# A hybrid attention block on one core: h written over the transposed x, row copies moved to another ring, and three steps set some ticks later

## The chip, the core and the metric

The kernel runs on one core of one Trainium2 chip. The metric is the device time of one execution in microseconds (us); the time of a version is the median of its runs. The core has a matrix engine (TensorE, PE in the rows), a vector engine (VectorE, DVE), a scalar engine (ScalarE, ACT), a general engine (GpSimd, POOL) and a sync engine (SyncE, SP) whose only work here is to issue transfers. Each engine takes its own instructions in order; semaphores hold them back where they depend on one another.

## What is computed

One residual block for a sequence of 1024 tokens and 1024 channels, in float32. Cut to what matters here:

```python
mod = silu(c) @ ada_w + ada_b                       # adaLN: six vectors of 1024
shift1, scale1, gate1, shift2, scale2, gate2 = split(mod, 6)
h = rms_norm(x, pre_mix_w) * (1 + scale1) + shift1
proj = h @ w_in                                     # q, k, v, gates of both branches
o_a = gla_chunked(...)                              # 4 heads, gated and normed
o_d = gated_delta_chunked(...)                      # 8 heads (GDN), gated and normed
merged = sigmoid(m_a) * (o_a @ w_branch_gla) + sigmoid(m_d) * (o_d @ w_branch_gdn)
x = x + gate1 * rms_norm(merged @ w_out, post_mix_w)
h2 = rms_norm(x, pre_mlp_w) * (1 + scale2) + shift2
x = x + gate2 * rms_norm(square(relu(h2 @ mlp_w1)) @ mlp_w2, post_mlp_w)
```

## The kernel before

**Precision.** A product in float32 is made of three matmuls in a rounded format: a high part times a high part, low times high, high times low. So every operand is split: ACT casts the high part (`hH`, `wH`, `oH`), DVE subtracts it from the original to get the low part (`hL`, `wL`, `oL`). Where the weights come by an accumulating transfer, ACT writes the negated high part and POOL's queue adds the weights to it.

**Memory.** Most tiles come from four rings in SBUF: `w4` with 30 slots of 128x1024 floats, `wt` with 8, `hd` with 4, `sl` with 2 (lines 24, 75 to 78). A new tile takes a slot whose last tenant is released, and its first writer waits for every reader of that tenant, a transfer out of it among them.

**Order.** A clock of ticks counts the PE's work: `tick` (line 377) is called after every few matmuls, `at(n, fn)` (line 366) puts a step n ticks ahead, and `run_due` puts the steps that are due into the engines' queues at that place. A tick says only where an instruction stands in its engine's queue, not when it runs. For the stage of the branch products `st(t, fn)` counts ticks from `stage0`, and tables such as `gla_plan` (line 1588) list the steps.

**The start.** x comes in as eight row tiles, is normed and transposed by PE into `xT[0..7]`, one tile of channels each. The first two adaLN vectors (shift1 and scale1) are made in four passes, p = 0 to 3, each for the channels of two tiles. The weights of pass 0 lie in `hd` (`ada_load`, line 200), those of pass 1 in `sl` and `wt`, those of passes 2 and 3 in `w4`. A pass is: `ada_pe` (16 matmuls into one bank), `ada_out` (ACT copies the 128x512 result to a row tile `acc`), `ada_fin` (PE sums it into columns), `ada_cols` (DVE makes the columns `am1`, `sh1`), `high` (ACT writes `hH` of both tiles from `xT`), `low` (line 279: DVE writes `h` = xT * am1 + sh1, then `hL` = h - hH, and SP stores `h` to HBM in `h_d`, where a later stage reads it). `first_tiles` (line 485) interleaves these passes with the first matmuls of h with the weights: `a_` (hH by high weights), `b_` (hH by low weights), `c_` (hL by high weights); the table `fill` gives the three groups that stand within each pass.

**The middle.** Then come key tiles, a triangular solve, branch gates, the four GLA heads, and the eight GDN heads (`gdn_head`, line 898), the last of which runs into the next stage. A GDN head ends with: `results` (ACT squares and copies the output to `ob`), `norm` and `scale` (DVE: a root in 11 small steps, then `ob` times it), `fin` (PE transposes `ob` half by half in four 128x128 pieces, DVE gates it into `sg`, printed as `si` in the rows), and a store to `od_d`. For head 6 these steps are set 27 ticks later (`end`), so that they stand in the products' stage, where they alternate with head 7's.

**The products.** `stage0` is the tick at which head 7's dense part ends and the branch products begin. Each of the three branches (GLA's, a gate's, GDN's) is made of seven half-size products in the order P2, P1, P6, P7, P4, P5, P3 (line 1755), 8 ticks each (48 matmuls with 512 columns in four groups of 12; the first two groups need the weights of half h = 0, the others those of h = 1). Operands are prepared by the plan: `x_cast`/`x_low` give `oH`/`oL`, `w_cast`/`w_low` the two parts of `wB` (halves h = 0 and 1). `split_raw` (line 1584) puts `w_cast` and, two ticks later where no accumulating transfer is used, `w_low`. P4 of the GLA branch starts at tick 32.

**adaLN's other four vectors** are summed on DVE throughout the heads, one piece every 12 ticks (`ada_sum`, line 1333), and closed by `ada_total` (line 1343): transposes and sums on DVE in two parts, one PE step 14 ticks later, DVE columns, and for the gates a row that goes to HBM.

Of the kernel before, what the change touches and what calls it, by code (L numbers as in the profile page):

```python
# [9 lines left out]
F32R = mybir.dt.float32r  # L10
# [40 lines left out]
def block_kernel(ctx: ExitStack, tc: tile.TileContext, x, c, ada_w, ada_b, pre_mix_w, post_mix_w,  # L51
# [9 lines left out]
    w4 = ctx.enter_context(tc.tile_pool(name="w4", bufs=1))  # L61
# [9 lines left out]
    def nm(p):  # L71
        uid[0] += 1
        return f"{p}{uid[0]}"
# [3 lines left out]
    def t4(shape=(128, 1024), dt=F32, p="t", tag="w4"):  # L77
        return w4.tile(list(shape), dt, tag=tag, name=nm(p), bufs=tag_bufs[tag])
# [4 lines left out]
    def pat(shape=(128, 512)):  # L83
        return pa.tile(list(shape), F32, tag="pa", name=nm("pa"))

    def dump(name, src, dst=None):
        if dbg and name in dbg:
            DMA.dma_start(dbg[name] if dst is None else dst(dbg[name]), src)
# [20 lines left out]
    def small(n, p="s", bufs=3, dt=F32):  # L109
        return sm.tile([128, n], dt, tag=f"{p}{n}", name=nm(p), bufs=bufs)  # L110
# [111 lines left out]
    xT = [t4(p="xT") for _ in range(8)]  # L222
# [21 lines left out]
    accs, pac, pcol = {}, {}, {}  # L244
# [7 lines left out]
                     start=(k < 4), stop=(k >= 4))  # L252

    def ada_out(p):
        accs[p] = t4((128, 512), p="acc")
        A.copy(accs[p], pac[p])

    def ada_fin(p):
# [11 lines left out]
    hH, hL, hs = [None] * 8, [None] * 8, [None] * 8  # L270
# [7 lines left out]

    def low(p):
        for d in (2 * p, 2 * p + 1):  # L280
            hs[d], hL[d] = t4(p="h"), t4(dt=F32R, p="hL")
            V.tensor_scalar(hs[d], xT[d], am1[:, d:d + 1], sh1[:, d:d + 1], ALU.mult, ALU.add)
            V.tensor_tensor(hL[d], hs[d], hH[d].bitcast(F32), ALU.subtract)
            DMA.dma_start(h_d[d // 2][d % 2], hs[d])
            dump("hT", hs[d], lambda t, d=d: t[d * 128:(d + 1) * 128, :])
# [80 lines left out]
    def at(dt, fn):  # L366
        agenda.append((clock[0] + dt, len(agenda) + uid[0] * 100000, fn))
        agenda.sort(key=lambda e: e[:2])
        uid[0] += 1
# [49 lines left out]
    def conv_w_later(raw_ap, shape, dh, dl, src=None):  # L419

        w = [None, None]

        def high():
            w[0] = t4(shape, F32R, "wH", "wt")
            A.copy(w[0], raw_ap)

        def low():
            w[1] = t4(shape, F32R, "wL", "wt")
            if src is None:
                V.tensor_tensor(w[1], raw_ap, w[0].bitcast(F32), ALU.subtract)  # L430
            else:
                A.activation(w[1], raw_ap, AF.Copy, scale=-1.0)
                G.dma_start(w[1], src, accum_op=ALU.add)

        at(dh, high)
        at(dl, low)
        return w
# [47 lines left out]
    def first_tiles():  # L485
# [27 lines left out]

        wk_low(0)
        low(0)
        V.tensor_tensor(wS[:, :, 32:64], raw_lba, wS[:, :, 0:32].bitcast(F32), ALU.subtract)
        wk_low(1)
# [6 lines left out]
        for p in range(1, 4):  # L524
            f = [lambda e=e: e[0](*e[1:]) for e in fill[p]]
            ada_pe(p)
            ada_out(p)
            f[0]()
            ada_fin(p)
            ada_cols(p)  # L530
            high(p)
            f[1]()
            f[2]()
            low(p)
            if p == 2:
                ahead[1] = next(ahead[0])
            a_(p)
# [153 lines left out]
    def r3(t, n=8):  # L691
        return t.rearrange("p (t q) -> p t q", t=n)
# [205 lines left out]
    def gdn_head(h, then=None):  # L898
# [163 lines left out]
                on(47 + late if hf else 35, lambda: results(hf, po))  # L1062

        late, end = (7, 27) if h == 6 else (0, 0)
        f_ = end + 6 if h == 7 else end

        def results(hf, po):
            if not hf:
# [264 lines left out]
    def ada_sum(i, k, raw):  # L1333
        with V.behind():
            if k == 0:
                adat[i] = t4(p="aacc", tag="hd")
                V.tensor_scalar(adat[i], raw, sc[:, k:k + 1], None, ALU.mult)
            else:
                V.scalar_tensor_tensor(adat[i], raw, sc[:, k:k + 1], adat[i], ALU.mult, ALU.add)
        if k == 7:  # L1340
            at(28 if i == 3 else 8, lambda: ada_total(i))

    def ada_total(i):

        _, b0, w0, dst = ADA[i]
        acc, bias, z = adat.pop(i), adab[:, b0:b0 + 8], {}
        t, r = t4(p="sqt"), small(32, "asr", 2)

        def part(hf):
            h_ = slice(hf * 512, (hf + 1) * 512)  # L1350
            with V.behind():
                V.transpose(t[:, h_], acc[:, h_])
                V.reduce_sum(r[:, hf * 16:(hf + 1) * 16], r3(t[:, h_], 16), axis=mybir.AxisListType.X)

        def total():
            z["ps"] = pat()
            T.matmul(z["ps"][:, 0:32], quad.rearrange("p a b -> p (a b)"), r, start=True, stop=True)

        def columns():
            o = small(8, "gcol", 1) if dst is None else dst  # L1360
            for c in range(4):
                q = slice(32 * c, 32 * c + 32)
                V.tensor_tensor(o[q], z["ps"][q, 0:32].rearrange("p (t c) -> p c t", c=4)[:, c], bias[q], ALU.add)
            if dst is None:
                V.tensor_tensor(o, o, vcol[:, w0:w0 + 8], ALU.mult)
                at(10, lambda: ada_row(i, o))
            elif dst is am2:
                V.scalar_tensor_tensor(am2, am2, 1.0, premlp, ALU.add, ALU.mult)

        part(0)  # L1370
        at(2, lambda: part(1))
        at(14, total)
        at(15, columns)

    def ada_row(i, g):
        ps, row = pat(), sm.tile([128, 256], F32, tag="gst", name=nm("grow"), bufs=3)[:, 0:128]
        T.transpose(ps[0:8, 0:128], g, ident)
        V.tensor_copy(row[0:8], ps[0:8, 0:128])
        ST.dma_start(gw_d[i // 3].rearrange("(r p) -> r p", p=128), row[0:8])
# [180 lines left out]
    A11, A12, A21, A22 = (0, 0), (1, 0), (0, 1), (1, 1)  # L1560
# [8 lines left out]
    def rows_of(r, gated=True):  # L1569

        for kp in range(2):
            r += [(25 + kp, "x_sum", Q21, Q21, "t2", kp),
                  (26 + kp, "x_cast", "P4", Q21, kp), (27 + kp, "x_low", "P4", Q21, kp),
                  (33 + kp, "x_cast", "P5", Q12, kp), (34 + kp, "x_low", "P5", Q12, kp),
                  (41 + kp, "x_cast", "P3", Q22, kp), (42 + kp, "x_low", "P3", Q22, kp)]
        for h in range(2):
            r += [(32 + 2 * h, "w_cast", "P5", A21, h), (36 + 2 * h, "w_low", "P5", A21, h),
                  (38 + 4 * h, "w_cast", "P3", A12, h), (44 + 3 * h, "w_low", "P3", A12, h)]
        for (cb, tb), t in (((0, 0), 13), ((1, 0), 37), ((1, 1), 45), ((0, 1), 53)):
            for h in range(2 if gated else 0):  # L1580
                r += [(t + 4 * h - 6, "load_s", cb, tb, h)]
        return sorted(r, key=lambda e: e[0])

    def split_raw(r, p, key, c0, c1, dma=True):
        for h, c_ in ((0, c0), (1, c1)):
            r += [(c_, "w_cast", p, key, h), (c_ + 1 + (not dma), "w_neg" if dma else "w_low", p, key, h)]

    def gla_plan():
        r = [(-19, "load_w", A12, True), (-16, "load_x", Q21, "wt"), (-11, "load_w", A11, True), (-5, "load_x", Q11),
             (-4, "load_x", Q12), (-3, "load_x", Q22), (-2, "load_w", A21), (1, "add_w", A21, A22), (8, "load_w", A22),  # L1590
             (21, "load_x", Q21)]
        split_raw(r, "P2", A12, -10, -7)
        split_raw(r, "P1", A11, -3, 1)
        split_raw(r, "P4", A22, 22, 25, False)
        for kp in range(2):
            r += [(-6 + kp, "x_cast", "P2", Q21, kp), (-5 + kp, "x_low", "P2", Q21, kp),
                  (-1 + kp, "x_cast", "P1", Q11, kp), (kp, "x_low", "P1", Q11, kp),
                  (1 + kp, "x_sum", Q12, Q12, Q11, kp), (3 + kp, "x_t2", kp), (5 + kp, "x_sum", Q11, "t2", Q11, kp),
                  (8 + kp, "x_cast", "P6", "t2", kp), (9 + kp, "x_low", "P6", "t2", kp),
                  (8 + 2 * kp, "w_sum", A11, A21, A11, kp), (10 + kp, "w_cast", "P6", A11, kp), (12 + kp, "w_low", "P6", A11, kp),  # L1600
                  (14 + kp, "w_sum", A12, A12, A11, kp), (15 + kp, "w_sum", A11, A22, A11, kp),
                  (17 + kp, "x_cast", "P7", Q11, kp), (18 + kp, "x_low", "P7", Q11, kp),
                  (19 + kp, "w_cast", "P7", A11, kp), (20 + kp, "w_low", "P7", A11, kp)]
        return rows_of(r)
# [651 lines left out]
    for n in range(len(seq)):  # L2256
        gi, key, c = seq[n]
        grp = GROUPS[gi]
        first, end = c == grp[0], c == grp[-1]
# [58 lines left out]
    for t in range(NT):  # L2318
        hf, to = t // 4, slice(t % 4 * 128, t % 4 * 128 + 128)
        end = t == NT - 1  # L2320
# [43 lines left out]
```

## Time and profile before

| what | us |
|---|---|
| median of 3 runs | 1916.46 |
| lowest and highest of them | 1913.89 and 1917.49 |
| the profiled execution | 1914.38 |
| its span, first to last instruction | 1912.7 |
| PE busy in the span | 1879.5 |

The profile is one execution. A row of the timeline has the start, the duration, the engine, the operation with what it writes and reads, the count, and in brackets the idle time just before it and what ended it. PEld is the loading of weights into the matrix engine, which runs beside the matmuls. Matmuls overlap, so the time that a group takes is read from the start of one row to the start of the next. Names have no buffer numbers in the profile; in the order of instructions they have, so that a tile can be followed there. All these instructions are recorded through one helper and so carry one line number; the tile names tell them apart.

### The profile page before, as it was taken

Reading aid. Unit: us, or ns where it says so; the run is one execution under the profiler, and the core shown is the slowest. Engines: PE = TensorE matmul, PEld = TensorE weight load, DVE = VectorE, ACT = ScalarE, POOL = GpSimd, SP = SyncE. Lnnn points to the kernel's source line nnn. Section 1 sums busy time; section 2 is a strip of 40 time slices with the busy share of each in tenths; the row PEclk is TensorE's granted clock in tenths of the full one; section 3 lists DMA queues with packets and bytes.
Section 4 is the critical chain, followed back from the end, with each engine's and each line's share of the span. In section 5 each row is a group of like instructions: output and inputs, shape, how many; then the busy total and the mean of one; then the engine's idle time right before and its main releaser. Section 6 shows DMA issues by size and latency. Waiting matters only on the chain.

```text
span 1912.7 us, 26562 instructions
## 1 busy us (share of the span) xinstructions
PE 1879.5 (98%) x10217; PEld 1576.4 (82%) x10217; DVE 1352.7 (71%) x2178; ACT 884.6 (46%) x1613; POOL 150.8 (8%) x140
## 2 busy tenths in 40 slices
PE   6999999999999999999999999999999999999998
PEld 4788888889898888888878888888888888888886
DVE  5564744769775666766788678667578886777887
ACT  5465324342432444444654556457544446443333
POOL 2020020110101000000101011000012120000001
PEclk9899999999999999999999999999999999999999
DMA  9485773122224444444869567436666758262425
GB/s 320 163 251 171 194 161 101 56 89 90 76 91 147 120 132 132 134 138 126 254 169 231 178 174 206 134 101 201 220 207 221 245 204 307 100 220 87 178 100 99
DMA packets 251567, 312.23 MB, mean 163 GB/s; under 512 B 72530, under 2 KB 178208, under 8 KB 251440
## 3 DMA queue, kind: packets, MB, share of 16 engines
q1 hardware_dynamic: 221936, 274.67, 44.8%
q0 software_dynamic: 13232, 20.85, 6.2%
q10 hardware_dynamic: 16272, 15.02, 2.4%
q8 instruction: 80, 1.31, 0.3%
q14 instruction: 47, 0.39, 0.1%
HBM read 230.10 MB, written 80.39 MB: 162 GB/s over the span
## 4 chain that ended last, share of the span: by engine, by line
PE 95%; DMA 2%; DVE 2%; ACT 1%; issue 0%; POOL 0%; DVEq 0%; ACTq 0%; SPq 0%; POOLq 0%
PE pm L38 62%; PE pa L38 33%; DMA wq<-in_w_branch_gla_dram 1%; DMA h_d<-h 1%; DMA vt<-in_c_dram 0%; DVE oL L38 0%; DVE rt L38 0%; ACT hH L38 0%; ACT ob L38 0%; DVE ob L38 0%; DVE hL L38 0%; DVE rs L38 0%; DVE ya L38 0%; ACT jk L38 0%; DVE wL L38 0%
## 5 line engine op out<-in xcount | busy, mean ns | idle before, releaser
L38 PE MATMUL pm<-hH,wH 128*128 128x512 f32 x864 | 286.3, 412 | 0.0
L38 PE MATMUL pm<-hL,wH 128*128 128x512 f32 x864 | 268.6, 392 | 0.0
L38 PE MATMUL pm<-hH,wL 128*128 128x512 f32 x864 | 267.2, 390 | 0.0
L38 PE MATMUL pm<-oH,wB 128*128 128x512 f32 x672 | 215.7, 395 | 0.0
L38 PE MATMUL pa<-w,yH 128*128 128x512 f32 (+1 forms) x696 | 212.3, 387 | 0.0
L38 PEld LDWEIGHTS pm<-hH,wL 128*128 128x128 f32 x864 | 162.1, 188 | 36.4
L38 PEld LDWEIGHTS pm<-hL,wH 128*128 128x128 f32 x864 | 162.2, 188 | 36.1
L38 DVE TENSOR_TENSOR w<-raw,w 128x512 fp32r<-128x512 f32 (+1 forms) x144 | 125.8, 876 | 49.4 <-ACT w L38 48.5
L38 PEld LDWEIGHTS pm<-hH,wH 128*128 128x128 f32 x864 | 145.1, 190 | 17.0
L38 PEld LDWEIGHTS pa<-w,yH 128*128 128x128 f32 x696 | 130.1, 188 | 26.8 <-DVE ya L38 0.4
L38 PEld LDWEIGHTS pm<-oH,wB 128*128 128x128 f32 x672 | 126.7, 189 | 26.4 <-DMA wB<-in_w_branch_gla_dram 0.4
L38 ACT CAST w<-raw 128x512 fp32r<-128x512 f32 (+1 forms) x144 | 99.3, 711 | 89.1 <-DVE raw L38 79.2
L38 PE MATMUL pa<-w,yL 128*128 128x512 f32 (+1 forms) x348 | 134.5, 387 | 0.0
L38 PE MATMUL pm<-oL,wB 128*128 128x512 f32 x336 | 131.3, 391 | 0.0
L38 PE MATMUL pa<-oB,w 128*128 128x512 f32 x480 | 111.4, 390 | 0.0
L38 ACT CAST wH<-raw 128x1024 fp32r<-128x1024 f32 x62 | 64.5, 1048 | 93.2 <-PE pm L38 45.9
L38 PEld LDWEIGHTS pa<-oB,w 128*128 128x128 f32 x480 | 89.8, 188 | 18.5
L38 DVE SCALAR_TENSOR_TENSOR cv<-pm,ccol,cv 128x1023 f32<-128x1023 f32 (+2 forms) x72 | 92.1, 1279 | 14.8 <-ACT cv L38 11.7
L38 DVE TENSOR_TENSOR wL<-raw,wH 128x1024 fp32r<-128x1024 f32 x62 | 76.2, 1233 | 35.6 <-ACT wH L38 35.5
L38 PE MATMUL pm<-oT,w 128*128 128x512 f32 x384 | 90.8, 389 | 0.0
L38 PE MATMUL pa<-oT,w 128*128 128x512 f32 x384 | 90.8, 389 | 0.0
L38 DVE TENSOR_TENSOR ya<-pa,ya 128x512 f32<-128x512 f32 (+1 forms) x83 | 56.0, 683 | 43.7 <-PE pa L38 43.7
(378 smaller groups left out, 3711.1 us busy)
## 6 DMA issues: line engine op xcount, KB each, us to landing
yL<-y_d SPq DMA_DIRECT2D x53, 512.0 KB, 7.5
raw<-in_mlp_w_dram SPq DMA_DIRECT2D x23, 1024.0 KB, 6.2
raw<-in_w_in_dram SPq DMA_DIRECT2D x18, 1024.0 KB, 7.3
raw<-in_w_in_dram SPq DMA_DIRECT2D x32, 512.0 KB, 4.8
araw<-in_ada_w_dram SPq DMA_DIRECT2D x32, 512.0 KB, 3.8
raw<-in_mlp_w_dram SPq DMA_DIRECT2D x18, 512.0 KB, 5.4
araw<-in_ada_w_dram SPq DMA_DIRECT2D x32, 256.0 KB, 6.0
sl<-sg_d SPq DMA_DIRECT2D x16, 512.0 KB, 7.9
```

What stands on the lines that cost most here:

```text
L38: r = fn(*args, **kw)
```

## The change

Five edits, and nothing else:

```diff
     def ada_out(p):
-        accs[p] = t4((128, 512), p="acc")
+        accs[p] = t4((128, 512), p="acc", tag="hd" if p else "w4")
         A.copy(accs[p], pac[p])
...
     def low(p):
         for d in (2 * p, 2 * p + 1):
-            hs[d], hL[d] = t4(p="h"), t4(dt=F32R, p="hL")
+            hs[d], hL[d] = xT[d], t4(dt=F32R, p="hL")
             V.tensor_scalar(hs[d], xT[d], am1[:, d:d + 1], sh1[:, d:d + 1], ALU.mult, ALU.add)
             V.tensor_tensor(hL[d], hs[d], hH[d].bitcast(F32), ALU.subtract)
             DMA.dma_start(h_d[d // 2][d % 2], hs[d])
...
         late, end = (7, 27) if h == 6 else (0, 0)
-        f_ = end + 6 if h == 7 else end
+        f_ = end + {6: 5, 7: 6}.get(h, 0)
...
         if k == 7:
-            at(28 if i == 3 else 8, lambda: ada_total(i))
+            at(40 if i == 3 else 8, lambda: ada_total(i))
...
-    def split_raw(r, p, key, c0, c1, dma=True):
+    def split_raw(r, p, key, c0, c1, dma=True, lag=2):
         for h, c_ in ((0, c0), (1, c1)):
-            r += [(c_, "w_cast", p, key, h), (c_ + 1 + (not dma), "w_neg" if dma else "w_low", p, key, h)]
+            r += [(c_, "w_cast", p, key, h), (c_ + (1 if dma else lag), "w_neg" if dma else "w_low", p, key, h)]
...
-        split_raw(r, "P4", A22, 22, 25, False)
+        split_raw(r, "P4", A22, 22, 25, False, 4)
```

The row copies of passes 1 to 3 take slots of `hd`, whose first tenants are the weights of pass 0. h takes no slot of its own. Head 6's `fin` moves by five ticks, the last adaLN total by twelve, and the two low parts of the GLA branch's P4 weights by two. No arithmetic is added or removed.

**First place: the passes at the start, on ACT.** The rows around the copy `acc` of pass 2, with the semaphores that each waits for. SP's transfers use eight semaphores in turn, named DMAHW0 to 7. Before:

```order
L38 COPY acc_539<-pa_530 128x512 [waits PE_49,Activation_49]
L38 ACTIVATE hH_553<-xT_189,sh_125,am_126 128x1024 [waits DVE_49]
L38 COPY acc_596<-pa_587 128x512 [waits DMAHW4_49,PE_49]
L38 ACTIVATE hH_610<-xT_191,sh_125,am_126 128x1024 [waits DVE_49,Activation_49]
L38 CAST wH_632<-raw_182 128x1024 [waits DMAHW3_49]
L38 COPY acc_657<-pa_648 128x512 [waits DMAHW6_49,DMAHW5_49,PE_49]
```

And after:

```order
L38 COPY acc_537<-pa_528 128x512 [waits PE_49]
L38 ACTIVATE hH_551<-xT_189,sh_125,am_126 128x1024 [waits DVE_49]
L38 COPY acc_592<-pa_583 128x512 [waits DMAHW3_49,PE_49]
L38 ACTIVATE hH_606<-xT_191,sh_125,am_126 128x1024 [waits DVE_49]
L38 CAST wH_626<-raw_182 128x1024 [waits DMAHW3_49]
L38 COPY acc_651<-pa_642 128x512 [waits DMAHW5_49,DMAHW4_49,PE_49]
```

DMAHW4 is, at this point before, the semaphore of SP's 45th transfer, the first store of `h`. After, the tenants before the copies are weights of pass 0 (SP's 9th to 16th transfers, where DMAHW3 belongs to the 12th and DMAHW4 and 5 to the 13th and 14th).

**The same place on DVE.** `low` of pass 2 and what follows it. Before:

```order
L38 TENSOR_SCALAR h_622<-xT_191,am_126,sh_125 128x1024 [waits DMAHW5_49,DVE_49]
L38 TENSOR_TENSOR hL_623<-h_622,hH_610 128x1024 [waits DVE_49,Activation_49]
L38 TENSOR_SCALAR h_627<-xT_192,am_126,sh_125 128x1024
L38 TENSOR_TENSOR hL_628<-h_627,hH_612 128x1024 [waits DMAHW3_49,DMAHW4_49,DVE_49,Activation_49]
L38 TENSOR_TENSOR wL_633<-raw_182,wH_632 128x1024 [waits DMAHW3_49,DMAHW7_49,DMAHW0_49,Activation_49]
```

And after:

```order
L38 TENSOR_SCALAR xT_191<-xT_191,am_126,sh_125 128x1024 [waits Activation_49]
L38 TENSOR_TENSOR hL_618<-xT_191,hH_606 128x1024 [waits DVE_49]
L38 TENSOR_SCALAR xT_192<-xT_192,am_126,sh_125 128x1024 [waits Activation_49]
L38 TENSOR_TENSOR hL_622<-xT_192,hH_608 128x1024 [waits DMAHW4_49,DVE_49]
L38 TENSOR_TENSOR wL_627<-raw_182,wH_626 128x1024 [waits DMAHW3_49,DMAHW7_49,DMAHW0_49,Activation_49]
```

The write over `xT` now waits for ACT, which reads the same tile for `hH`; before, only the subtraction waited for it. `hL_622` waits for DMAHW4, the first store of `h`, as `hL_628` did.

**Second place: head 6's end, on DVE.** Before (`ob_8432` and `si_8231` are head 6's, `si_8670` is head 7's; `wB_9054` is the second half of P4's weights, `oL_9066` and `oL_9092` P4's inputs, `sqt` and `asr` the last adaLN total):

```order
L38 TENSOR_TENSOR wB_9054<-wq_8795,wB_9053 128x1024
L38 TENSOR_TENSOR oL_9066<-xq_8995,oH_9065 128x1024
L38 TENSOR_TENSOR oL_9092<-xq_8997,oH_9091 128x1024
L38 STREAM_TRANSPOSE sqt_9101<-aacc_7202 128x512
L38 TENSOR_REDUCE asr_9102<-sqt_9101 128x16
L38 TENSOR_TENSOR ob_8432<-ob_8432,rs_9078 128x1024
L38 STREAM_TRANSPOSE sqt_9101<-aacc_7202 128x512
L38 TENSOR_REDUCE asr_9102<-sqt_9101 128x16
L38 SCALAR_TENSOR_TENSOR si_8231<-pa_9134,vcol,si_8231 128x512
L38 SCALAR_TENSOR_TENSOR si_8231<-pa_9147,vcol,si_8231 128x512
```

And after, from P4's inputs (`oL_9058`, `oL_9083`) on; head 6 has `ob_8424` and `si_8223`, head 7 `si_8662`, and P4's second weights are `wB_9045`:

```order
L38 TENSOR_TENSOR oL_9058<-xq_8987,oH_9057 128x1024
L38 TENSOR_TENSOR oL_9083<-xq_8989,oH_9082 128x1024
L38 TENSOR_TENSOR ob_8424<-ob_8424,rs_9070 128x1024
L38 TENSOR_TENSOR wB_9045<-wq_8787,wB_9044 128x1024
L38 TENSOR_TENSOR oL_9142<-xq_8595,oH_9141 128x1024
L38 TENSOR_TENSOR oL_9154<-xq_8597,oH_9153 128x1024
L38 SCALAR_TENSOR_TENSOR si_8662<-pa_9159,vcol,si_8662 128x512
L38 TENSOR_TENSOR wB_9129<-wq_8630,wB_9128 128x1024
L38 SCALAR_TENSOR_TENSOR si_8662<-pa_9173,vcol,si_8662 128x512
L38 SCALAR_TENSOR_TENSOR z_9207<-sl_9120,pm_8794 128x1024
L38 SCALAR_TENSOR_TENSOR si_8223<-pa_9185,vcol,si_8223 128x512
```

`ob` of head 6 stands right behind P4's inputs, and its two gatings stand among P5's preparations; the adaLN total follows further down. P4's first low weights, which stood ahead of head 7's norm, stand between the two sums that make P4's inputs. On PE head 6's two sets of four transposes, which stood one tick before the end of P7 and at P4's start, now stand behind the first half of P4, after head 7's two sets. On SP and POOL no instruction changes its place.

## The prediction

> **What bounds the kernel now.** The page first: one engine is busy nearly throughout.
>
> ```profile
> span 1912.7 us, 26562 instructions
> PE 1879.5 (98%) x10217; PEld 1576.4 (82%) x10217; DVE 1352.7 (71%) x2178; ACT 884.6 (46%) x1613; POOL 150.8 (8%) x140
> ```
>
> PE is idle for 1912.7 - 1879.5 = 33.2 us in all. No matmul is removed, so only this idle time, and matmuls that run slowly, can be won. The list of waits of PE alone says where it sits:
>
> ```profile
> PE pm L38 <- POOL onesR L38: 9.9, 1, 9.9
> PE pa L38 <- ACT acc L38: 7.8, 2, 7.0
> PE pa L38 <- DVE ob L38: 3.9, 1, 3.9
> ```
>
> The first is the program's start, before any matmul, and the change doesn't touch it. The second and third are single waits of 7.0 and 3.9 us, and both are named in the change. The chain of waits shows what stands behind the longer one:
>
> ```profile
> 40.30 0.70 DVE hL L38
> 41.00 9.59 DMA h_d<-h
> 50.66 0.59 ACT acc L38
> 51.30 1.86 PE pa L38 x8
> ```
>
> The copy `acc` of pass 2 waits until the first store of `h` has landed: it took that tile's slot in `w4`. Its source was ready long before. The busy time by stretches shows a second price, in the granted clock (the column before the DMA share):
>
> ```profile
> 50.00:55.00 5.00, 3.70 (x13) 3.31 (x14) 1.21 (x5) 1.86 (x3) 0.00 (x0) 0.50 0.47 190
> 55.00:60.00 5.00, 5.00 (x16) 3.61 (x15) 4.31 (x4) 2.04 (x2) 0.00 (x0) 0.65 0.51 210
> 1000.00:1005.00 5.00, 1.52 (x7) 1.34 (x8) 4.93 (x7) 0.00 (x0) 0.00 (x0) 0.90 0.43 127
> 1005.00:1010.00 5.00, 5.00 (x21) 4.06 (x20) 2.84 (x4) 3.23 (x4) 0.00 (x0) 0.76 0.75 197
> ```
>
> After each gap PE is "busy" at 0.50 to 0.76 of its clock. So each gap costs more than its length.
>
> **The first place: acc and h.** PE's timeline, passes 2 and 3:
>
> ```profile
> 41.22 1.92 PE L38 MATMUL pa<-araw,one 128*32 128x512 f32 x16
> 43.08 1.20 PE L38 MATMUL pm<-hH,w 128*128 128x512 f32 x4
> 51.30 1.86 PE L38 MATMUL pa<-onesR,acc 128*128 128x1 f32 x8 [7.03 <-ACT acc L38]
> ...
> 60.33 1.92 PE L38 MATMUL pa<-araw,one 128*32 128x512 f32 x16
> 62.18 1.20 PE L38 MATMUL pm<-hH,w 128*128 128x512 f32 x4
> 63.22 0.95 PE L38 MATMUL pa<-onesR,acc 128*128 128x1 f32 x8
> 64.02 1.11 PE L38 MATMUL pa<-hL,wS 128*64 128x512 f32 x4
> ...
> 69.75 1.98 PE L38 MATMUL pm<-hL,w 128*128 128x512 f32 x8
> 71.56 2.01 PE L38 MATMUL pa<-hL,wS 128*64 128x512 f32 x8
> ```
>
> Pass 2 takes from 41.22 to 60.33, 19.1 us. Pass 3 shows what the same work takes undisturbed: 16 matmuls 1.85, four with the low weights 1.04, `ada_fin` 0.80; a full matmul takes (71.56 - 69.75) / 8 = 0.226, so eight `c_` take 1.81 and the twelve of `a_` 2.72. Sum 8.2 us: pass 3 would start at 49.4, **10.9 us** earlier, of which 7.0 are the gap and 3.9 the slow matmuls.
>
> The Trainium skill (TensorE: Matmul & The Clock Gate, What's actually happening) has the clock halve after an idle window of about 3.4 us and return after a busy one of the same length. By that a gap would cost 3.4 / 2 = 1.7 us more; the trace has 3.9 after the first gap and agrees in kind alone. With 1.7 at both gaps the sum of this prediction would be 7.0 + 3.9 + 3.4 = 14.3 us, and the sum itself goes by the rows.
>
> Does the copy then start at once? Its slot in `hd` was last read by pass 0's matmuls, over long before. ACT's next steps, by pass 3:
>
> ```profile
> 62.34 0.59 ACT L38 COPY acc<-pa 128x512 f32<-128x512 f32 x1 [5.31 <-PE pa L38]
> 64.66 2.38 ACT L38 ACTIVATE hH<-xT,sh,am 128x1024 fp32r<-128x1024 f32 x2 [1.73 <-DVE sh L38]
> ```
>
> The copy starts 2.01 after `ada_pe`, so at 43.2, and `ada_fin` at 44.1. hH starts 1.44 after that (45.55) and is ready at 46.7 and 47.9; `a_` reaches the two tiles at 46.7 and 48.1. It just fits, as it does in pass 3.
>
> What is late next? Two loads and one store, issued before 42 us and not moved:
>
> ```profile
> 40.20 0.37 SPq L38 DMA_DIRECT2D raw<-in_w_in_dram  x1
> DMA to landing us min/median/max: 5.3/7.2/9.0
> DMA to landing us min/median/max: 2.6/5.9/10.5
> ```
>
> (The first landing line is that of the `raw` tiles, the second that of the stores `h_d`.) The raw weights are down by 49.2, and ACT's cast of them by 50.3, ahead of pass 3's copy at 49.4 + 2.0 = 51.4. The first store, landed at 50.6, now holds DVE's `hL_622`, behind which `wL` and pass 3's `am`, `sh` are queued, and for these PE waits: 50.6 and two operations (a pair takes 2.35 in the row of `oL` below) make 52.95, against 53.3, when `ada_fin` gives them their input. So 0.35 us are left. The copy's wait is gone, but the same landing is the next to matter.
>
> h over xT: the same eight DVE instructions, now in place.
>
> ```profile
> L38 DVE TENSOR_SCALAR x<-x,rs x8: 734/748/857, 8.9 to 20.5; 128x1024 f32<-128x1024 f32 x8
> 27.44 0.81 DVE L38 TENSOR_SCALAR h<-xT,am,sh 128x1024 f32<-128x1024 f32 x1
> ```
>
> The scaling of x already runs in place in 0.75 us, so I take 0.81 as it is; an unhidden step that ran at the pace of a two-input operation (1.22) would add 0.4 on DVE. The new wait is for ACT's read of `xT`: a low part, ready 1.2 us after its hH before, is ready some 2.0 after it now. PE uses low parts one pass later or at the end (`c_(2,0)` stands at about 58.8, `hL_622` is ready at 51.8, `hL` of the last tile at 58.9 and used about 59.7), so they stay hidden; cover gone, it would cost 0.8 us once. First place: 10.9, of which I take **10.8 us** since hH only just fits; between 8.5 (landings some 2.5 us later) and 11.
>
> **The second place: head 6's end.**
>
> ```profile
> 999.16 0.39 PE L38 MATMUL pm<-oH,wB 128*128 128x512 f32 x1
> 1003.48 0.68 PE L38 MATMUL pa<-ident,ob 128*128 128x128 f32 x4 [3.93 <-DVE ob L38]
> ...
> 1010.15 0.60 PE L38 MATMUL pa<-ident,ob 128*128 128x128 f32 x4
> 1010.51 0.48 PE L38 MATMUL pm<-oH,wB 128*128 128x512 f32 x1
> ```
>
> From 999.4, the end of that last matmul (999.16 + 0.23), to 1010.15 PE does two sets of transposes and 18 matmuls: at full pace 2 x 0.36 + 18 x 0.226 = 4.8 of 10.75 us. So the wait costs **5.9 us**, 2.0 of them slow matmuls. Why `ob` is late stands on DVE:
>
> ```profile
> 988.08 1.23 DVE L38 TENSOR_TENSOR wB<-wq,wB 128x1024 fp32r<-128x1024 f32 x1 [2.39 <-ACT wB L38]
> 994.23 1.22 DVE L38 TENSOR_TENSOR ob<-ob,rs 128x1024 f32<-128x1024 f32 x1
> 998.60 2.35 DVE L38 TENSOR_TENSOR oL<-xq,oH 128x1024 fp32r<-128x1024 f32 x2
> 1002.21 1.22 DVE L38 TENSOR_TENSOR ob<-ob,rs 128x1024 f32<-128x1024 f32 x1
> 1019.47 1.22 DVE L38 SCALAR_TENSOR_TENSOR z<-sl,pm 128x1024 f32<-128x1024 f32 x1 [0.83 <-PE pm L38]
> ```
>
> DVE works through from 988 to 1003 and head 6's `ob` (1002.21) is last. After: P4's first `wB`, which stood at 988.08 where DVE had just idled, now stands between the sums, +1.14; the second leaves the space ahead of `oL`, -1.14. So `oL` stays at 998.6, ready at 999.8 and 1000.9. PE, without the transposes, begins P4 six matmuls after 999.4, at 1000.8, and its second pair of k at 1002.1: 1.0 and 1.2 us to spare. `ob` of head 6 follows at 1000.9 to 1002.0; its transposes are due after P4's first half, past 1006. The second `wB` is ready at 1003.2, due at about 1007. The total's two parts (together some 2.7 us of DVE) go behind these.
>
> Then DVE has no pause any more: `oL` twice, two `wB`, four gatings, `z`, two sums and half the total fill it from 1003.2 to about 1015, so the second `z` ends at about 1016.5 (1019.47 before). It must be done when the second half of P5 takes that bank, about 1018.6. This is the next thing late, by a margin of 2 us. Second place: **5.9 us**, between 2 and 6. Two things move past other queues and cost nothing that I can see: head 6's store to `od_d` is issued five ticks later on ACT's queue, some 50 ticks ahead of its reader, and the last adaLN row goes out later, to be read at the program's very end.
>
> **Sum.** 10.8 + 5.9 = 16.7 us. Against the profiled execution, 1914.38 - 16.7 = 1897.7; its time is 2.1 under the median of the runs, so for the median 1916.46 - 16.7 = **1899.8 us**. Nothing later waits for a fixed moment: after the second place the list of PE's waits is empty, so what is won is kept unless a transfer sets the pace.
>
> **Rivals.** *The landing stays the gate.* DVE's `hL_622`, `am` and PE behind it wait for the first store as `acc` did. For it: only 0.35 us of room, and its 9.6 us to landing were near the slowest of the stores (10.5). Against: the transfers ahead of it are the same. With a landing 4 us later: 3.6 us of gap and about 2 of slow matmuls come back, 1916.46 - 11.1 = 1905.4.
>
> *DVE takes over at the second place.* PE waits for P4's `oL` or for the second `z`. For it: DVE has no idle time left there. Against: the margins of 1.0 to 2.0 us. A gap above 3 us would bring back all 5.9: 1905.7.
>
> *The slow time after a gap was long by chance.* The first gap cost 3.9 us of slow matmuls, the second 2.0. If the clock comes back at a moment that varies, and a usual execution loses 2.0 at both, the executions behind the median have 1.9 less to win: 16.7 - 1.9 = 14.8, so 1901.7. For it: 5.00 us at 0.65 as late as 55 to 60. Against: the profiled execution, with that loss in it, was faster than the median. The Trainium skill (TensorE: Matmul & The Clock Gate, What's actually happening) speaks for it: its window runs freely, so that the moment varies from run to run; no two profiles here can show that.
>
> *What is won is waited for again (the same, or slower).* Where the products of the gate's branch begin, POOL's accumulating weight transfers must land before PE arrives:
>
> ```profile
> 1033.62 1.28 POOL L38 DMA_DIRECT2D wB<-in_w_in_dram  x1 [6.01 <-ACT wB L38]
> DMA to landing us min/median/max: 6.1/8.0/10.7
> ```
>
> The one of 1033.62 lands by 1044.3 at the latest, and PE needs it 28 ticks (of six matmuls, 1.36 us) after P4's start at about 1006.9, at some 1046: 1.7 us to spare. If the transfers set the pace there and keep their moments while PE comes 5.9 us earlier, PE waits 4.2 us, and 2.0 more for the slow matmuls behind the gap. If all four halves of these weights fall behind by as much, each after the last, that is 4 x 6.2 = 24.8, more than the 16.7 won, and 1916.46 + 8.1 = 1924.6. It decides from a landing 1.7 us later, against PE, than now; with three such gaps (18.6) the time is about that of before. Against: POOL waits for ACT there, and ACT for PE's release of slots, so these transfers move up with PE.
>
> **Chances.** Forecast 0.66; the landing 0.10; DVE at the second place 0.12; the shorter slow time 0.06; waited for again, 0.04 the same and 0.02 slower. All but the last two are faster by over 0.2% (3.8 us, about what a measurement of this kernel can tell from no change): 0.94 faster, 0.04 the same, 0.02 slower. The range goes from the lowest run with 17.7 us won (1913.89 - 17.7 = 1896.2) to 1906.0, which takes in the two rivals at 1905.4 and 1905.7; 0.06 of the chances lie past it, and some for an error in a term.
>
> **What would show it.** In the changed kernel's list of PE's waits the 7.0 behind `acc` and the 3.9 behind `ob` are gone, the granted clock is near 1.0 from 45 to 60 and around 1000, pass 3's `ada_pe` starts near 49.4, and P4 starts without a gap. Wrong would be: a wait of PE on `am` or hH near 53 (the landing), a wait on `oL` or on P5's banks, or new waits of PE on `wB` behind transfers later on.

## The result and the profile after

| what | us |
|---|---|
| before, median of 4 runs | 1916.24 (1913.89 to 1917.49) |
| after, median of 4 runs | 1898.84 (1898.38 to 1899.62) |
| profiled executions, before and after | 1914.38 and 1898.38 |
| their spans | 1912.7 and 1896.7 |

After against before the ratio is 0.9911 with a 95% interval of [0.9894, 0.9928]: faster, by 17.4 us between the medians and by 16.0 us between the two profiled executions. 1899.8 was forecast, and 16.7 us for the sum. Of all the executions told of here one stands apart, 4776.4 us for the kernel with 2 MB more traffic, for a cause that the record does not show; it is left out of that kernel's median below.

The page of the changed kernel has the shorter span and nearly the same work on every engine:

```profile
span 1896.7 us, 26550 instructions
PE 1873.9 (99%) x10217; PEld 1572.4 (83%) x10217; DVE 1351.1 (71%) x2178; ACT 884.0 (47%) x1613; POOL 154.5 (8%) x140
```

The list of PE's waits (total, times, longest) no longer has 7.0 us behind `acc`, nor 3.9 behind `ob`. Besides the program's start (the first row; the list names another releaser for it than before) only waits of 0.8 us and less are left:

```profile
PE pm L38 <- DVE x L38: 10.0, 1, 10.0
PE pm L38 <- ACT hH L38: 1.1, 3, 0.6
PE pa L38 <- ACT acc L38: 0.8, 1, 0.8
```

The busy time by stretches, at the two places (the granted clock stands before the DMA share): no stretch is slow.

```profile
50.00:55.00 5.00, 5.00 (x35) 2.99 (x35) 2.84 (x5) 1.03 (x3) 1.70 (x3) 1.00 0.92 377
55.00:60.00 5.00, 4.73 (x21) 3.31 (x20) 3.97 (x4) 2.06 (x2) 0.00 (x0) 1.00 0.37 149
995.00:1000.00 5.00, 5.00 (x30) 4.20 (x29) 5.00 (x7) 0.00 (x0) 1.28 (x1) 1.00 1.08 324
1000.00:1005.00 5.00, 5.00 (x24) 4.13 (x23) 4.97 (x7) 2.23 (x3) 1.28 (x1) 1.00 0.97 227
```

PE's timeline in the first place: pass 2 begins at 41.36, its column sums at 44.24 without a wait, its `c_` at 45.05 and `a_` at 46.99, pass 3 at 49.95 (60.33 before), and the low parts follow at 59.77 (69.75 before).

```profile
41.36 1.92 PE L38 MATMUL pa<-araw,one 128*32 128x512 f32 x16
44.24 0.95 PE L38 MATMUL pa<-onesR,acc 128*128 128x1 f32 x8
45.05 2.09 PE L38 MATMUL pm<-hL,w 128*128 128x512 f32 x8
46.99 0.73 PE L38 MATMUL pm<-hH,w 128*128 128x512 f32 x2
49.95 1.92 PE L38 MATMUL pa<-araw,one 128*32 128x512 f32 x16
55.98 0.72 PE L38 MATMUL pm<-hH,w 128*128 128x512 f32 x2 [0.27 <-ACT hH L38]
59.77 1.52 PE L38 MATMUL pm<-hL,w 128*128 128x512 f32 x6
```

DVE there. The first store of h still holds somebody back: DVE's `hL`, for 0.62 us. But behind it DVE waits 1.01 us for PE, so PE does not wait for that landing.

```profile
48.96 0.81 DVE L38 TENSOR_SCALAR xT<-xT,am,sh 128x1024 f32<-128x1024 f32 x1
50.38 1.23 DVE L38 TENSOR_TENSOR hL<-xT,hH 128x1024 fp32r<-128x1024 f32 x1 [0.62 <-DMA h_d<-xT]
53.84 0.16 DVE L38 TENSOR_TENSOR am<-pa,vcol 128x2 f32<-128x2 f32 x1 [1.01 <-PE pa L38]
```

In the second place head 6's `ob` is ready at 990.52 + 1.21 = 991.7, and its transposes (the second pair of rows; the first pair is head 7's) come at 996.78 and 998.61, 5 us later and without a wait:

```profile
990.52 1.21 DVE L38 TENSOR_TENSOR ob<-ob,rs 128x1024 f32<-128x1024 f32 x1
1004.71 1.21 DVE L38 SCALAR_TENSOR_TENSOR z<-sl,pm 128x1024 f32<-128x1024 f32 x1
```

```profile
993.12 0.60 PE L38 MATMUL pa<-ident,ob 128*128 128x128 f32 x4
994.96 0.60 PE L38 MATMUL pa<-ident,ob 128*128 128x128 f32 x4
996.78 0.60 PE L38 MATMUL pa<-ident,ob 128*128 128x128 f32 x4
998.61 0.60 PE L38 MATMUL pa<-ident,ob 128*128 128x128 f32 x4
```

So of the 16.0 us between the spans some 10.0 come from the first place (69.75 - 59.77) and 6.0 from the second. That is an attribution from two executions; the experiments take the places apart.

### The profile page after: what moved, and what is told of

Read it like the earlier page. It is cut to its first block, busy times and chain, and to the rows that moved or that the text cites. A ratio compares the mean times of both kernels' runs of the same rounds, so it can differ in the third digit from the quotient of the medians.

```text
span 1896.7 us, 26550 instructions
## 1 busy us (share of the span) xinstructions
PE 1873.9 (99%) x10217; PEld 1572.4 (83%) x10217; DVE 1351.1 (71%) x2178; ACT 884.0 (47%) x1613; POOL 154.5 (8%) x140
## 4 chain that ended last, share of the span: by engine, by line
PE 96%; DMA 2%; DVE 1%; SPq 1%; ACT 0%; issue 0%; DVEq 0%; ACTq 0%
PE pm L38 63%; PE pa L38 33%; DMA wq<-in_w_branch_gla_dram 1%; DMA araw<-in_ada_w_dram 1%; SPq L38 1%; DMA x<-in_x_dram 0%; DVE oL L38 0%; DVE rt L38 0%; ACT ob L38 0%; DVE ya L38 0%; ACT jk L38 0%; DVE wL L38 0%; ACT hH L38 0%; DVE yg L38 0%; DVE raw L38 0%
```

## The experiments

Twelve kernels ran, the last of them the changed one once more, in four groups. The kernel before ran in every group; its medians were 1913.91, 1914.66, 1914.10 and 1914.30 us. "Won" is against the median of before in the same group. "Above the changed kernel" is against 1898.84 us, which comes from the first comparison; in the last group that kernel stood at 1898.06, so such a difference is uncertain by about 1 us.

**The two edits of the first place, each alone.** First the row copies only:

```diff
-        accs[p] = t4((128, 512), p="acc")
+        accs[p] = t4((128, 512), p="acc", tag="hd" if p else "w4")
```

> Only the row copies move to the ring hd; h keeps a slot of its own. Both parts needed (my theory): one slot fewer is taken from w4, and the slot that the first store of h holds falls to the second hH of pass 2 on ACT, which then waits for the landing at 50.6 and is ready at about 51.8, where PE wants it at 48.1. The wait of 7.0 us behind acc becomes one of about 3.7 behind hH, with some 1.5 to 2 us of slow matmuls: of the 10.4 us of the first place about 5 are won, 1911 us. Rival, the copies' ring alone does it: 10.4 won, 1906. Rival, it only renames the wait: 0 to 1 won, 1915 to 1916.

Measured: 1909.44 us, ratio 0.9973 [0.9962, 0.9984], 4.5 won. Then h over xT only:

```diff
-            hs[d], hL[d] = t4(p="h"), t4(dt=F32R, p="hL")
+            hs[d], hL[d] = xT[d], t4(dt=F32R, p="hL")
```

> Only h is written over xT; the row copies stay in w4. Both parts needed (my theory): acc of pass 2 takes another slot and goes at once, but the second hH of pass 2 now takes the slot that the first store holds, as with the other part alone: a wait of PE of about 3.7 us on hH, some 1.5 to 2 us of slow matmuls, about 5 us won, 1911 us. Rival, one part alone does it: 10.4 won, 1906. Rival, in place the store still holds the slot and nothing is won: 1916.

Measured: 1910.15 us, ratio 0.9980 [0.9971, 0.9989], 3.8 won. The ACT timeline with the row copies alone, at pass 2: the copy goes at once, and the second hH waits 3.62 us for the store.

```profile
43.60 0.59 ACT L38 COPY acc<-pa 128x512 f32<-128x512 f32 x1 [3.88 <-PE pa L38]
50.87 1.24 ACT L38 ACTIVATE hH<-xT,sh,am 128x1024 fp32r<-128x1024 f32 x1 [3.62 <-DMA h_d<-h]
```

With h over xT alone, the same instruction waits for the same store, now from xT:

```profile
51.44 1.24 ACT L38 ACTIVATE hH<-xT,sh,am 128x1024 fp32r<-128x1024 f32 x1 [4.37 <-DMA h_d<-xT]
```

PE then waits for this hH, 3.2 us in the one kernel (first row) and 3.9 in the other:

```profile
52.17 0.73 PE L38 MATMUL pm<-hH,w 128*128 128x512 f32 x2 [3.21 <-ACT hH L38]
```

```profile
52.73 1.22 PE L38 MATMUL pm<-hH,w 128*128 128x512 f32 x2 [3.94 <-ACT hH L38]
```

Each edit alone hands the occupied slot to the next tenant, hH; only both together hand it to DVE's `hL`, which has the time. Neither "one alone is enough" (10.4 won) nor "it only renames the wait" (1 or less) held.

**Each place alone.** The two edits above without the others:

> Both edits of the first place, none of the second. My theory: pass 3 starts 10.0 to 10.4 us earlier as in the changed kernel, and all of it reaches the end: 1916.2 - 10.2 = 1906.0 us, with the wait of 3.9 us behind ob as before. Rival, the two places are coupled (what is won at the start is partly waited for later without the other edits): under 8 won, over 1908.

Measured: 1904.21 us, ratio 0.9948 [0.9936, 0.9961], 9.7 won. And the other three edits without these two:

> The three edits of the second place, none of the first. My theory: the wait of 3.9 us behind ob goes and with it 2.0 us of slow matmuls: 1916.2 - 5.9 = 1910.3 us, and the wait of 7.0 us behind acc is as before. With the edits of the first place alone this adds up to the whole, 16 to 17.4 us. Rival, a usual execution loses less than 2 us to the slow matmuls: 4 to 5 won, 1911.5 to 1912.

Measured: 1908.25 us, ratio 0.9968 [0.9956, 0.9980], 5.7 won. Each kernel keeps the other place's wait, the first row in the kernel with the first place mended, the second in the other:

```profile
PE pa L38 <- DVE ob L38: 3.9, 1, 3.9
```

```profile
PE pa L38 <- ACT acc L38: 7.9, 2, 7.1
```

**Which edit carries the second place.** Only `fin`, against the kernel before:

```diff
-        f_ = end + 6 if h == 7 else end
+        f_ = end + {6: 5, 7: 6}.get(h, 0)
```

> Of the second place only head 6's fin is set five ticks later; DVE's order ahead of ob is as before. My theory: the transposes stand some 6.8 us later on PE, which covers the wait of 3.9 us by itself, so that ob can stay where it is: 5 to 6 us won, 1910 to 1911 us, as with all three edits of that place. Rival, the edits on DVE are needed (ob or the low parts behind it come late again, with P4's inputs or z waited for): under 3 won, over 1913.

Measured: 1909.06 us, ratio 0.9969 [0.9959, 0.9980], 5.6 won: as much as with all three. `ob` is ready even later than before, and PE has no wait on it, since its transposes stand past it:

```profile
1002.71 1.22 DVE L38 TENSOR_TENSOR ob<-ob,rs 128x1024 f32<-128x1024 f32 x1
```

```profile
1007.63 0.60 PE L38 MATMUL pa<-ident,ob 128*128 128x128 f32 x4
```

Only the two moves on DVE:

```diff
-            at(28 if i == 3 else 8, lambda: ada_total(i))
+            at(40 if i == 3 else 8, lambda: ada_total(i))
...
-        split_raw(r, "P4", A22, 22, 25, False)
+        split_raw(r, "P4", A22, 22, 25, False, 4)
```

> Of the second place only the two moves on DVE (the last adaLN total twelve ticks later, P4's second low weights two ticks later); fin stays. Worked out from the rows: two low-weight operations (1.14 each) and none of the total's parts ahead of ob in the old order, so ob is ready some 1.1 to 2.5 us earlier and PE still waits 1.4 to 2.8 us for it. If the clock is lost only behind gaps of more than about 3 us (my theory), the 2.0 us of slow matmuls go whole: 3.1 to 4.5 won, 1911.7 to 1913.1. Rival, slow matmuls in proportion to the gap (0.5 us for each): 1.7 to 3.7 won, with a granted clock under 0.95 right behind the gap.

Measured: 1911.72 us, ratio 0.9987 [0.9978, 0.9996], 2.9 won. PE's row:

```profile
1001.56 0.66 PE L38 MATMUL pa<-ident,ob 128*128 128x128 f32 x4 [2.61 <-DVE ob L38]
```

The wait is 1.3 us shorter, and in the profiled execution the granted clock is 1.00 throughout the place, so there the slow matmuls are gone whole, as I expected. The 2.9 us won are a little under the 3.1 to 4.5 that I gave, and inside the rival's range; the rival's other sign, a clock under 0.95 behind the gap, is not there. The reason I gave, a threshold in the gap's length, did not survive the next kernel.

**The gap's length and the clock.** The changed kernel with the row copy of pass 2 repeated, five or thirteen times (the edit for five; for thirteen 13 stands in place of 5):

```diff
-        A.copy(accs[p], pac[p])
+        for _ in range(5 if p == 2 else 1):
+            A.copy(accs[p], pac[p])
```

> The changed kernel with the row copy of pass 2 made five times instead of once (same result), so that ACT is some 4 x 0.6 = 2.4 us later with it and PE stands idle about 2.3 us at that place. If the clock drops only behind a longer gap (my theory): 1898.8 + 2.3 = 1901.1 us, granted clock 1.0 behind the gap. Rival, slow matmuls in proportion to the gap (3.9 for 7.0): 2.3 + 1.3, so 1902.4 us.

Measured: 1902.70 us (1902.13 to 1903.66), 3.9 above the changed kernel's 1898.84. My number was too low, the rival's near.

> The changed kernel with the row copy of pass 2 made thirteen times, so that PE stands idle about 12 x 0.6 = 7.2 us, as it did in the kernel before. If the profiled execution of before was a usual one (my theory): 7.2 + 3.9 us of slow matmuls, 1898.8 + 11.1 = 1909.9 us. Rival, the slow time was long by chance and a usual execution loses 1.7 to 2.0 us: 9.0, so 1907.8 us.

Measured: 1907.58 us (1906.61 to 1909.58), 8.7 above the changed kernel. Here the rival's number held too. The profiled execution is the slowest of the runs for both kernels, and shows what a run can lose. PE behind the gap of the five copies, and then the stretches of 3.4 us that follow the clock's own edges:

```profile
46.80 1.57 PE L38 MATMUL pa<-onesR,acc 128*128 128x1 f32 x8 [2.05 <-ACT acc L38]
48.24 3.76 PE L38 MATMUL pm<-hL,w 128*128 128x512 f32 x8
```

```profile
43.80:47.20 3.40, 1.35 (x8) 0.83 (x7) 0.00 (x0) 2.82 (x5) 0.00 (x0) 0.99 1.10 352
47.20:50.60 3.40, 3.40 (x12) 2.92 (x13) 0.84 (x4) 1.73 (x2) 0.00 (x0) 0.50 1.04 413
50.60:54.00 3.40, 3.40 (x10) 2.41 (x9) 3.33 (x4) 1.58 (x2) 0.00 (x0) 0.50 0.96 393
54.00:57.40 3.40, 3.40 (x24) 1.40 (x22) 1.34 (x2) 0.00 (x0) 0.47 (x2) 1.00 0.36 149
```

A gap of 2.05 us halved the clock for two such stretches, while the gap of 2.61 above, which lay across two of them (1.45 us idle in the first, 1.16 in the second), left it at 1.00:

```profile
997.00:1000.40 3.40, 1.95 (x9) 1.29 (x7) 3.23 (x9) 1.75 (x2) 0.00 (x0) 1.00 0.68 261
1000.40:1003.80 3.40, 2.24 (x15) 1.94 (x15) 2.90 (x3) 0.17 (x1) 0.00 (x0) 1.00 0.53 158
```

So neither a threshold in the gap's length nor a price in proportion to it fits both kernels. That what counts is how much of one stretch of 3.4 us is idle fits both; the last section comes back to it.

**The landing as the next gate.** The changed kernel with one transfer more on POOL's queue, which writes hH of the fourth tile to scratch memory, twice or four times over (the edit for twice, 1 MB; for four times, 2 MB, both 2s before 128 are 4s):

```diff
+    h_x = dr.tile([2, 128, 1024], F32, name="h_x")
...
+            if d == 2:
+                G.dma_start(h_x.rearrange("a p c -> p a c"), hH[3].bitcast(F32).unsqueeze(1).to_broadcast([128, 2, 1024]))
             DMA.dma_start(h_d[d // 2][d % 2], hs[d])
```

> The changed kernel with one more transfer on POOL's queue: hH of the fourth tile, written twice to scratch memory (1 MB), issued about when the first store of h is (41 us), so that this store shares the transfer engines and lands some 2 to 3 us later (1 MB at 350 GB/s is 3 us). DVE's hL of pass 2 waits for it. By the 0.35 us of room that I worked out before: PE waits about 2 us on am or hH of pass 3, 1901 us. By the 1.0 us that the changed kernel's trace shows: about 1.5 us, 1900.3. Rival, the landing gates nothing (other stores or loads have more room): within 0.3 of 1898.8.

Measured: 1900.71 us, 1.9 above the changed kernel. Ratio to before 0.9930 [0.9918, 0.9941].

> The same with 2 MB, so that the first store lands some 5 to 6 us later. With 1.0 us of room PE waits 4 to 5 us there and, as the gap is then over 3 us, loses some 2 us more to slow matmuls: 1898.8 + 6 to 7 = 1905 to 1906 us, the size of the rival that I called the landing stays the gate. Rival, the landing gates nothing: within 0.5 of 1898.8.

Measured: 1903.10 us (five runs, 1901.58 to 1904.85), 4.3 above. Ratio to before 0.9943 [0.9930, 0.9955]. With 1 MB more, DVE waits 2.80 us for the store, and PE 1.20 for hH of pass 3:

```profile
53.91 1.22 DVE L38 TENSOR_TENSOR hL<-xT,hH 128x1024 fp32r<-128x1024 f32 x1 [2.80 <-DMA h_d<-xT]
```

```profile
42.70 1.93 PE L38 MATMUL pa<-araw,one 128*32 128x512 f32 x16
58.30 0.73 PE L38 MATMUL pm<-hH,w 128*128 128x512 f32 x2 [1.20 <-ACT hH L38]
```

Counted from pass 2's start in each trace, `hL` begins 53.91 - 42.70 = 11.2 us in, against 50.38 - 41.36 = 9.0 in the changed kernel, and PE reaches these matmuls 15.6 us in, against 14.6. So the store was 2.2 us later and PE 1.0: 1.2 us of room, near the 1.01 that DVE's row shows. This execution took 2.3 us more than the changed kernel's profiled one. The other 1.3 us are the start of pass 2, 42.70 against 41.36, and they lie ahead of the added transfer, which was issued at 41.1: the passes had begun 0.5 us later, and in pass 1 PE had waited 0.38 and 0.50 us for loads of `araw`, and not 0.20 once. So the added transfer explains 1.0 us here, and how much of the medians' 1.9 is its work stays open. With 2 MB more the first wait of PE is another one:

```profile
53.83 1.04 ACT L38 CAST wH<-raw 128x1024 fp32r<-128x1024 f32 x1 [5.24 <-DMA raw<-in_w_in_dram]
54.78 0.58 ACT L38 COPY acc<-pa 128x512 f32<-128x512 f32 x1
```

```profile
55.41 1.05 PE L38 MATMUL pa<-onesR,acc 128*128 128x1 f32 x8 [1.87 <-ACT acc L38]
```

The load of the raw weights lands late too, ACT's cast of them waits, and pass 3's copy stands behind the cast. The gap of 1.87 us brings 3.4 us at half clock. Counted from pass 2's start, 41.89 here, `hL` begins at 55.23, 13.3 us in, so the store is 4.3 us later than in the changed kernel. So the transfers are the next gate, by the store first and, when they are later still, by the raw weights; the expected 6 to 7 us was too much.

**Three edits against five.** The changed kernel without its two moves on DVE, and the changed kernel once more beside it:

> The changed kernel without its two moves on DVE: row copies in hd, h over xT, and head 6's fin five ticks later. My theory after the single edits (fin alone won 5.6 us, all three of that place 5.7): these three edits carry all of the gain, 1898.8 us beside the whole change, within 0.5 us of it in the same call. Rival, the moves on DVE matter once the first place's gap is gone too (as all of DVE's steps then come in another phase with their transfers): over 1 us slower than the whole change.

> The changed kernel once more, beside the parts. The two places one at a time won 9.7 and 5.7 us, sum 15.4, while the change as a whole won 17.4 in its own comparison, where the kernel before stood at 1916.2 instead of 1913.9 to 1914.7. My theory: the kernel before scatters (1911.9 to 1917.5) because the clock's slow time behind its two gaps comes in steps of 3.4 us, and the changed kernel has none of it: it comes out at 1898.8 within 0.5 again, its runs within 1.5 of one another, and against the 17 runs of before of this call it wins 15 to 16. Rival, the places help one another by 2 us: 17 or more against the before of this call.

Measured: 1898.83 us (1897.84 to 1899.42), ratio 0.9919 [0.9905, 0.9932], with three edits; 1898.06 us (1897.44 to 1899.08), ratio 0.9917 [0.9903, 0.9930], with all five. The difference of 0.8 us is over the 0.5 I had allowed and under the rival's 1, and the ranges overlap: if the DVE moves bring anything on top, it is below what these runs can tell. Against the before of its own group the whole change wins 16.2 us, where the sum of the parts is 9.7 + 5.7 = 15.4; the intervals of the single ratios are wider than that difference, so no help of one place for the other is shown.

## Why the prediction was right, point by point

**What bounds the kernel.** PE's idle time and slow matmuls at two places: right. Both waits went, the clock stayed at 1.00, and no new wait of PE over 0.8 us came.

**First place, 10.8 us: 10.0 came.** The working was 8.2 us from `ada_pe` of pass 2 to that of pass 3; it took 49.95 - 41.36 = 8.6. The eight `c_` took 1.94 us and the twelve of `a_` 2.96, where 1.81 and 2.72 were taken: the price of one matmul in one row of eight was too low for these. The `a_` stand in groups that change every two or four matmuls, which may cost the rest; that is not tested. In pass 3 hH was 0.27 us late at 55.98, the step of which I had said that it only just fits, as it does in pass 3: in pass 2 it fits, in pass 3 not quite. And the start of pass 2 was 0.14 later in this execution (41.36 against 41.22), which the change doesn't touch.

**h over xT.** In place the scaling took 0.81 us, as taken; the wait for ACT's read is there and hidden.

**The landing next, 0.35 us of room: 1.0 to 1.2.** The mechanism is as written: the store holds `hL`, and `am` stands behind it. The size was off since the store was there at 50.38, 0.2 earlier than I took, and `am` got its input at 53.84, 0.5 later. The rival with a landing 4 us later did not come; made by hand, a delay of 4.3 us cost 4.3 us, less than the 5.6 I gave for it, and it came through the raw weights and ACT's cast of them, a path that the prediction took to be in time, ahead of pass 3's copy.

**What I saw only with the single edits:** the prediction treats the copy's ring and h in place as two things that happen together. They are worth 4.5 and 3.8 us apart and 9.7 together, because the occupied slot passes to the next tenant until it reaches one with time.

**Second place, 5.9 us: 5.7 alone, 6.0 between the two profiles.** The step at work is `fin` alone. The prediction gave the moves on DVE no gain of their own, and they have none that can be told once `fin` is later; without it they won 2.9. The second `z`, the step with a margin of 2 us, ended at 1005.9, 10.6 us before the 1016.5 worked out; 10.0 of these are what the first place had brought forward, and PE has no wait there.

**The slow time.** The sum took 3.9 and 2.0 us as fixed prices, and they vary from run to run. In the thirteen-copies kernel, which has the first gap again (6.99 us in its profile), a median run loses 8.7 - 7.0 = 1.7 us to slow matmuls (2.5 against the later median of 1898.06), if its gap is as long, and its profiled run 11.2 - 7.0 = 4.2. So the rival that called the slow time long by chance was right in kind. For the kernel before itself the record does not decide it. The change as a whole won 16.2 us in its own group, which leaves 16.2 - 7.0 - 3.9 = 5.3 for slow matmuls, nearer the sum's 5.9 than the rival's 4.0; the places one at a time leave 9.7 - 7.0 = 2.7 and 5.7 - 3.9 = 1.8, nearer the rival. And the first gap was itself 6.1 to 7.1 us long in the four profiles that have the passes as before, so that its length and the slow time behind it can't be told apart in the medians.

**From the profile to the median.** The 2.1 us between the profiled execution and the median of three runs was the scatter of the kernel before. Without them the forecast reads 1897.7, against 1898.84 and 1898.06. The 17.4 us of the first comparison are high for the same reason; 16.2 is the other value. So some luck is in the forecast's being within 1.0 us: the sum was 0.7 us more than the 16.0 between the profiled executions, and the 2.1 went the other way. Whether the scatter comes with the gaps is not shown: within a group of later runs the kernel before spans 2.0 to 5.2 us (9 to 17 runs) and the changed one 1.6 (5 runs), but in that last group it was 2.0 beside 1.6, and the kernel with 1 MB more traffic, whose profile has no slow time, spans 3.1.

**Waited for again, 0.06:** this did not come; the list of PE's waits has none over 0.4 us on a transfer of weights. The margin that I gave for it was too wide: 28 ticks of 1.36 us after 1006.9 are 1045.0, not 1046, which leaves 0.7 us after 1044.3 instead of 1.7.

## What to carry to other kernels

A wait for a ring's slot is mended only when the slot falls to a tenant that has the time: follow the slot to the next tenant before counting the wait as won. Price a gap of the matrix engine as its length plus a slow time that differs from run to run (0 to 4.2 us in the profiles here), and do not take the one profile's value as fixed. Of several edits at one place test the one that moves the waiting instruction by itself; here it carried the place.

## What the runs showed of the hardware

The time at half clock behind a gap came in steps of 3.4 us in every profile that has any: 10.2 us behind the gaps of 6 to 7 us (five kernels), 6.8 behind one of 3.9 and 3.4 behind one of 3.2 at the first place; 3.4 behind the gap of 3.9 at the second place in three kernels. In the kernel with only the first place mended the same gap of 3.9 cost two steps:

```profile
989.20:992.60 3.40, 0.36 (x2) 0.00 (x0) 3.37 (x5) 0.00 (x0) 0.00 (x0) 0.99 0.66 224
992.60:996.00 3.40, 2.50 (x8) 2.21 (x9) 2.81 (x4) 0.00 (x0) 0.00 (x0) 0.50 0.41 133
996.00:999.40 3.40, 3.40 (x11) 2.71 (x11) 1.33 (x2) 2.19 (x3) 0.00 (x0) 0.51 0.79 231
999.40:1002.80 3.40, 3.40 (x18) 2.79 (x18) 2.54 (x4) 2.71 (x3) 1.28 (x1) 1.00 1.04 342
```

The stretch from 992.60 has 0.9 us of idle time left at its start, and the next one is slow again; the clock returns after one that was busy throughout. With 2 MB more traffic it returned after a stretch with 0.28 us of idle time. This fits a decision at fixed edges, on what the stretch behind was filled with. The edges run on through the kernel: in the three kernels that have slow time at both places (the kernel before and the two with one edit of the first place), the clock records of the two first drops lie 955.73, 945.49 and 948.91 us apart, which are 280, 277 and 278 steps of 3.413 us. The Trainium skill (TensorE: Matmul & The Clock Gate, What's actually happening) has such a free-running window, of 3413 ns, and these steps agree with it. It has the clock drop after an idle window; here gaps of 1.87 and 2.05 us, each with eight matmuls of one column behind it, were enough, and 2.61 us split over two windows were not. How much a window may idle was not tried any finer. Why the fully busy stretch from 51.6 to 55.0 of the kernel before is followed by another slow one is open: it begins with those one-column matmuls (they follow the gap of 7.0 us until 53.0), which may count for little. The five-copies kernel fits that (they last until 48.24, inside the first of its two slow stretches), and so does the one with 2 MB more (they end before its only one), but it is only argued.

```profile
48.20:51.60 3.40, 0.30 (x2) 0.30 (x2) 0.00 (x0) 0.59 (x1) 0.00 (x0) 0.51 1.02 417
51.60:55.00 3.40, 3.40 (x13) 3.01 (x13) 1.21 (x5) 1.28 (x2) 0.00 (x0) 0.50 0.20 82
55.00:58.40 3.40, 3.40 (x10) 2.41 (x9) 3.31 (x4) 2.04 (x2) 0.00 (x0) 0.50 0.56 230
58.40:61.80 3.40, 3.40 (x25) 1.62 (x23) 1.00 (x1) 0.00 (x0) 0.00 (x0) 0.99 0.19 78
```
